# A decoder layer with 32 experts: the first expert's rows get a routing product of their own, and the last tile's bias sum becomes one of the planned tasks

## The chip, the cores and the metric

The kernel runs on 1 core of one Trainium2 chip. The metric is the device time of one execution in microseconds (us); lower is better. Three runs of the kernel before took 1487.82 to 1492.46 us, median 1490.6.

## What is computed

One layer of a decoder on 512 tokens of width 1024, all in float32. First a mixer (gated DeltaNet heads and sliding-window attention heads side by side) whose output is added to x. Then a mixture of experts: 32 experts, each token goes to its best 4. Cut to what matters here:

```python
h = _rmsnorm(x, norm2_w[l]) * (1.0 + scale2) + shift2
logits = xf @ w_router + b_router
top_val, top_idx = lax.top_k(logits, TOP_K)          # 4 of 32 experts per token
gates = jax.nn.softmax(top_val, axis=-1)
hu = xb @ w_up[e] + b_up[e]                          # xb: the rows of expert e
act = x_glu * sigmoid(SWIGLU_ALPHA * x_glu) * (x_lin + 1.0)
ys = act @ w_down[e] + b_down[e]
out = jax.ops.segment_sum(ys * row_gate[:, None], row_tok, num_segments=T)
x = x + gate2 * out
```

## The kernel before, in words

**Two phases.** The first phase computes the mixer and the routing, the second the experts. Between them the engines' orders are joined: what the first phase leaves on an engine's queue stands ahead of the second phase there.

**The first phase is planned.** Every piece of work is a generator that yields tuples of an engine ("P" TensorE, "V" VectorE, "S" ScalarE, "G" GpSimd, "D" a load on SyncE), an assumed cost in us, and buffer tags. `Flow.run` (L154) always picks the step that could start first by these costs, within a slack of 0.1 us the one with the lowest priority number, and emits its instructions. The order on each engine is the order of emission; the instructions then wait for their data with semaphores. A yielded list of keys waits until other tasks have marked them. After each step the next one of the same task becomes ready the engine's assumed latency later (0.12 for TensorE, 0.2 for the others).

**Routing.** The 512 tokens are four tiles of 128 rows. For tile i, `route(i)` (L1258) normalizes the rows, computes the logits, takes the top four (L1311 to L1316, the one-hot sum `ohs`), computes each row's position within its expert with products of TensorE (`pos`, L1320 to L1322), then on VectorE the softmax and the slot numbers (L1325 to L1331), and in `table` (L1179; L1183 to L1192 on VectorE, L1196 on TensorE) a table from slot and expert to token and gate, which is added up over the tiles in `ten` (L1342). `ranks` (L1497) counts the rows of each expert and sorts the experts by count (L1504 to L1517, `perm`); `eri` (L1524) is the list of experts in that order. Expert 0 is always first. `places` (L1529) needs `ten` of all tiles and `perm`: it writes `gi` (L1537), the token numbers of each expert's slots, and the rows and gates of the outputs (L1544 to L1550).

**Bias sums.** `finish(i)` (L1350) multiplies a tile's gates with the experts' down-biases (a transpose L1363, two products L1370, VectorE's product L1373), adds them to the residual rows (L1377, for the last tile on VectorE, else on GpSimd) and stores them to the output (L1381, for the last tile on ScalarE's queue, else on GpSimd's). For tiles 0 to 2 it is a planned task; for the last tile it is run behind the planned phase (L1666).

**The second phase.** Experts go in a fixed order of slots; for each, GpSimd clears a buffer and gathers the rows with an indirect DMA (`gather`, L1685), TensorE transposes them (L1706; VectorE copies the first half, ScalarE the second, L1707), multiplies by the up weights in eight steps (L1755), VectorE and ScalarE compute the activation (L1764 to L1770), TensorE transposes it (L1778), and the down product follows (L1792). TensorE's order is: up of expert q, with the activations of q-1 transposed before its fourth step and the rows of q+1 before its sixth, then down of q-1. Where an expert has few rows, its second unit of 64 rows is skipped in most steps.

**The weights** (1 MB chunks, 8 for up and 4 for down) come through SyncE's queue into a ring of 16 slots. The 12 chunks of the first expert are loaded during the first phase. The second expert's number is copied by GpSimd from `eri` into `second` (L1899), by an order edge behind the first gather, and SyncE reads it (L1877) before it issues that expert's chunks; behind six of them it issues the biases of the first two experts (L1635). For later chunks it waits until TensorE has released a slot.

**Another order edge** (L1903, `behind`) holds the last tile's two stores behind ScalarE's half of the first copy.

Of the kernel before, what the change touches and what calls it, by code (L numbers as in the profile page):

```python
# [12 lines left out]
I32 = mybir.dt.int32  # L13
# [170 lines left out]
def layer_kernel(ctx: ExitStack, tc: tile.TileContext, A, out, probe=None):  # L184
# [111 lines left out]
    def behind(late, early):  # L296

        tc.add_manual_dep(late.ins, early.ins.name,
                          mybir.DependencyInfo(mybir.DependencyClass.NoSync, mybir.DependencyReason.DATA), reason="order")
# [958 lines left out]
    def route(i):  # L1258
# [3 lines left out]
        rt = wk("cv", "rt", 4)  # L1262
        pay, t3, lTs = rt[:, 0:256], rt[:, 0:P].rearrange("p (k e) -> p k e", e=NE), rt[:, P:2 * P]
        cuts = {"at": 256}
        for n, w in (("lo", NE), ("v8", 8), ("g4", 8), ("ss", 4), ("i4", 4)):
            a = cuts["at"]
            cuts[n], cuts["at"] = rt[:, a:a + w], a + w
        lo, v8, g4, ssb, i4 = (cuts[n] for n in ("lo", "v8", "g4", "ss", "i4"))
        oh = oha[:, i]
        yield "N", 0.0, "x"  # L1270
        h2 = wk("x", "h2", 4, D)
# [49 lines left out]
            TE.matmul(pos, lhsT=bc(one, [P, P]), rhs=ohs[:, q], start=(q == 0), stop=False)  # L1321
        TE.matmul(pos, lhsT=C("LT"), rhs=ohs[:, i], start=(i == 0), stop=True)  # L1322
        S.activation(g4[:, 0:4], v8[:, 0:4], AF.Exp, bias=g4[:, 4:5], accum_out=g4[:, 5:6])
        yield "V", 1.0
        V.reciprocal(g4[:, 5:6], g4[:, 5:6])  # L1325
        V.tensor_scalar(slots[:, i, 1], g4[:, 0:4], g4[:, 5:6], None, op0=OP.mult)
# [162 lines left out]
    cnti = const.tile([NE, NE], I32, name="cnti")  # L1489
    ngr = (32 * NBMAX + P - 1) // P  # L1490
    gi = const.tile([P, ngr, NE], I32, name="gi")
    pieces = ((64, NBMAX // 2), (32, (NBMAX + 1) // 2))
    si = {w: const.tile([P, n, NE], I32, name=f"si{w}") for w, n in pieces}
    sg = {w: const.tile([P, n, NE], F32, name=f"sg{w}") for w, n in pieces}
# [65 lines left out]
    with tc.manual_schedule(engines={nc.vector.engine, nc.scalar.engine, nc.tensor.engine, nc.gpsimd.engine, nc.sync.engine}):  # L1560
        columns(rows2, 32, 51)
        for i in range(NT):
            (V.tensor_copy if i % 2 else S.copy)(swt[i // 2][:, i % 2, 0:512], tq[i])
        for i in range(2):
            (V.tensor_copy if i % 2 else S.copy)(swt[i][:, :, 512:768], tkv[i].rearrange("p (i n) -> p i n", n=256))

        def chain(*tasks):
            for t in tasks:
                yield from t

        def swa():
            flow.add(PR["swa"], swa_norms())
            for i in range(NT):
                flow.add(PR["swa"], swa_heads(i))
                for kv in range(2):
                    flow.add(PR["swa"], swa_weights(i, kv))
                    flow.add(PR["swa"] - 1, swa_values(i, kv))
            yield [("norms",)]

        order = [(n, p, c0 + 256 * p) for p in range(2) for n, c0 in (("k", 512), ("q", 0), ("v", 1024))]  # L1580
        flow.add(1, gates())
        wins[512, 0] = wins[512, 1] = w0s
        for hf in range(2):
            flow.mark("win", 512, hf)
        flow.taken.update({"x": 2, "r": 1})
        flow.free["V"] = 1.9
        flow.add(0, chain(*(win(c0) for c0 in [c for _, _, c in order][1:] + [1536, 1536 + 256])))
        flow.add(PR["conv"], chain(*(conv(p, n, c0, PR["cend"]) for n, p, c0 in order)))
        for p in range(2):
            for f in (lengths, decay, turned, inverse, levels):  # L1590
                flow.add(PR["in"] + (f is levels), f(p))
        flow.add(PR["swa"], swa())
        flow.add(1, late_loads())
        flow.add(PR["late"], chain(*(late(r) for r in range(2, 6))))
        flow.add(PR["z"], chain(*(gate(p, PR["z"]) for p in range(2))))
        flow.add(PR["load"], loads())
        flow.add(PR["rec"], recur())
        for i in range(NT):
            flow.add(PR["yS"], out_swa(i))
            flow.add(PR["yT"], out_delta(i))  # L1600
            flow.add(PR["rt"] - 0.2 * i, route(i))
            if i < NT - 1:
                flow.add(PR["fin"], finish(i))
        flow.add(PR["rt"], router_bias())
        flow.add(PR["rt"] - 0.1, ranks())
        flow.add(0, places())
        flow.run()
# [55 lines left out]
    ahead = (load_up(ahead[0]), load_down(ahead[1]))  # L1663

    see("oT", state["oT"].rearrange("p h t -> p (h t)"))
    for _ in finish(NT - 1):  # L1666
        pass
    mix.close()


# [14 lines left out]
    def gather(n, gidx):  # L1685
        xs = []
        for g in range((n + 3) // 4):
            rows_ = 32 * min(4, n - 4 * g)
            xg = moe.tile([P, D], F32, name="xg", bufs=3)
            xs.append((xg, rows_))  # L1690

            G.memset(xg[:rows_], 0.0)  # L1692
            state["gather"] = G.indirect_dma_start(  # L1693
                out=xg[:rows_], out_offset=None, in_=h2d, in_offset=bass.IndirectOffsetOnAxis(ap=gidx(g)[:rows_], axis=0),
                bounds_check=T - 1, oob_is_err=False)
        return xs
# [193 lines left out]

    def rows_of(q):
        r = ORDER[q]
        return gather(NB[r], lambda g: gi[:, g, r:r + 1])

    overflow = overflow_list()
    with tc.manual_schedule(engines={nc.sync.engine, nc.tensor.engine, nc.vector.engine, nc.scalar.engine}):
# [3 lines left out]
        ups = {0: ahead[0], 1: fetch_up(1)}  # L1900
        xs[1] = rows_of(1)
        xT = {0: turn(xs.pop(0))}
        for d in stores[-2:]:  # L1903
            behind(d, state["turned", 1])
        bbs = {0: spread_bias(NB[ORDER[0]], bias[0])}
        acts, pend, last = {}, [], {}
        for q in range(NE + 1):
# [88 lines left out]
```

## Time and profile before

| | |
|---|---|
| median of 3 runs | 1490.6 us (1487.82 to 1492.46) |
| the profiled execution | 1486.96 us, its span 1485.2 us |
| TensorE busy in the span | 1379.4 us (93%) |
| VectorE, ScalarE, GpSimd busy | 563.7, 237.7, 261.1 us |
| moved by DMA | 476.16 MB, 321 GB/s on average |
| mean granted TensorE clock | 0.977 |

The profile's engines are PE (TensorE products), PEld (its weight loads), DVE (VectorE), ACT (ScalarE), POOL (GpSimd) and SP (SyncE, which only issues DMAs here; "SPq" is its queue). Times are in us from the span's start. A row of the timeline gives the start, the duration, engine, line, operation, the tile written and the tiles read, the shape, the count of merged instructions, and in brackets how long the engine had been idle before and what ended that.

### The profile page before, as it was taken

Reading aid. Unit: us, or ns where it says so; the run is one execution under the profiler, and the core shown is the slowest. Engines: PE = TensorE matmul, PEld = TensorE weight load, DVE = VectorE, ACT = ScalarE, POOL = GpSimd, SP = SyncE. Lnnn points to the kernel's source line nnn. Section 1 sums busy time; section 2 is a strip of 40 time slices with the busy share of each in tenths; the row PEclk is TensorE's granted clock in tenths of the full one; section 3 lists DMA queues with packets and bytes.
Section 4 is the critical chain, followed back from the end, with each engine's and each line's share of the span. In section 5 each row is a group of like instructions: output and inputs, shape, how many; then the busy total and the mean of one; then the engine's idle time right before and its main releaser. Section 6 shows DMA issues by size and latency. Waiting matters only on the chain. (4 is left out here: it accounts for less than half of the span.)

```text
span 1485.2 us, 22293 instructions
## 1 busy us (share of the span) xinstructions
PE 1379.4 (93%) x8586; PEld 599.5 (40%) x8586; DVE 563.7 (38%) x1247; ACT 237.7 (16%) x542; POOL 261.1 (18%) x216
## 2 busy tenths in 40 slices
PE   4999999999878999879999999999999999999974
PEld 3766656754443333222233333333333333343311
DVE  7965577566753312212231232222331323232310
ACT  4353354431111000000000000000000000010000
POOL 2213143102331111100011101102010102211010
PEclk9999999999969999999999999999999999999986
DMA  9656210266447999999999999999999999999995
GB/s 304 208 199 213 102 44 15 64 214 269 142 174 287 389 401 404 397 401 415 411 411 400 385 423 402 385 407 397 400 368 364 387 350 405 390 417 415 414 415 236
DMA packets 104980, 476.16 MB, mean 321 GB/s; under 512 B 13992, under 2 KB 39556, under 8 KB 55714
## 3 DMA queue, kind: packets, MB, share of 16 engines
q1 hardware_dynamic: 91842, 453.16, 77.0%
q0 software_dynamic: 11952, 18.75, 5.4%
q10 hardware_dynamic: 1072, 2.70, 0.5%
q8 instruction: 75, 1.23, 0.3%
q14 instruction: 39, 0.32, 0.1%
HBM read 464.14 MB, written 17.22 MB: 324 GB/s over the span
## 5 line engine op out<-in xcount | busy, mean ns | idle before, releaser
L1755 PE MATMUL ps_up<-we,xTe 128*64 128x512 f32 (+1 forms) x3040 | 621.0, 605 | 22.7 <-DMA we<-in_w_up_dram 19.7
L1755 PEld LDWEIGHTS ps_up<-we,xTe 128*64 128x64 f32 (+1 forms) x3040 | 188.0, 132 | 395.5 <-issue 332.7
L1792 PE MATMUL ps_dn<-we,aT 128*64 128x512 f32 (+1 forms) x1848 | 316.9, 535 | 24.5 <-DMA we<-in_w_down_dram 13.9
L1792 PEld LDWEIGHTS ps_dn<-we,aT 128*64 128x64 f32 (+1 forms) x1848 | 103.4, 130 | 239.4 <-issue 185.3
L1800 POOL DMA_INDIRECT out_dram<-yv,si x52 | 81.7, 1571 | 655.0 <-DVE yv L1799 472.9
L1707 DVE COPY xTe<-ps_xTe 128x256 f32<-128x256 f32 (+3 forms) x35 | 17.5, 500 | 309.3 <-PE ps_xTe L1706 309.3
L1780 ACT COPY aT<-ps_aT 128x512 f32<-128x512 f32 (+1 forms) x52 | 26.0, 529 | 517.7 <-PE ps_aT L1778 514.2
L1764 DVE TENSOR_TENSOR hu<-ps_up,bb 128x512 f32<-128x512 f32 (+1 forms) x52 | 32.1, 617 | 200.0 <-PE ps_up L1755 200.0
L1799 DVE SCALAR_TENSOR_TENSOR yv<-ps_dn,sg,g2p 128x512 f32<-128x512 f32 x38 | 28.5, 751 | 193.9 <-PE ps_dn L1792 193.0
L1766 ACT ACTIVATE hu<-hu 128x512 f32<-128x512 f32 (+1 forms) x52 | 29.8, 573 | 271.3 <-DVE hu L1765 271.3
L1692 POOL MEMSET xg<- 64x1024 f32 (+3 forms) x35 | 37.1, 1080 | 188.9 <-PE ps_xTe L1706 188.6
L317 PE MATMUL ps_ch<-hhi,wih 128*128 128x512 f32 x128 | 58.3, 455 | 0.0
L317 PE MATMUL ps_ch<-hl,wih 128*128 128x512 f32 x128 | 50.6, 396 | 0.0
L317 PE MATMUL ps_ch<-hhi,wl 128*128 128x512 f32 x128 | 50.3, 393 | 0.0
L1715 DVE STREAM_SHUFFLE bb<-bias 128x1024 f32<-128x1024 f32 (+1 forms) x44 | 48.6, 1132 | 0.1
L1707 ACT COPY xTe<-ps_xTe 128x256 f32<-128x256 f32 (+3 forms) x35 | 15.2, 433 | 165.2 <-PE ps_xTe L1706 165.2
L1693 POOL DMA_INDIRECT xg<-h2d,gi x35 | 35.8, 1022 | 16.1 <-POOL xg L1692 8.3
L1706 PEld LDWEIGHTS ps_xTe<-cst,xg 64*128 64x128 f32 (+3 forms) x280 | 24.1, 142 | 32.6 <-issue 23.1
L1778 PEld LDWEIGHTS ps_aT<-cst,act 128*128 128x128 f32 x180 | 24.3, 208 | 29.3 <-issue 25.6
L1706 PE MATMUL ps_xTe<-cst,xg 64*128 64x64 f32 (+3 forms) x280 | 30.2, 250 | 5.4 <-DMA xg<-h2d,gi 2.5
L1142 PE MATMUL ps_y<-wos,oS 128*128 128x512 f32 x64 | 33.4, 613 | 0.0
L1778 PE MATMUL ps_aT<-cst,act 128*128 128x128 f32 x180 | 31.2, 304 | 2.3 <-DVE act L1770 1.9
(392 smaller groups left out, 1378.6 us busy)
## 6 DMA issues: line engine op xcount, KB each, us to landing
we<-in_w_up_dram SPq DMA_DIRECT2D x256, 1024.0 KB
we<-in_w_down_dram SPq DMA_DIRECT2D x128, 1024.0 KB
wa<-in_w_ada_dram SPq DMA_DIRECT2D x16, 512.0 KB
wi<-in_w_in_dram SPq DMA_DIRECT2D x8, 1024.0 KB
wl<-in_w_ada_dram SPq DMA_DIRECT2D x12, 512.0 KB
oS<-in_w_ada_dram SPq DMA_DIRECT2D x10, 512.0 KB
LL<-in_w_ada_dram SPq DMA_DIRECT2D x10, 512.0 KB
wt<-in_w_in_dram SPq DMA_DIRECT2D x4, 776.0 KB
```

What stands on the lines that cost most here:

```text
L317: TE.matmul(acc, lhsT=w[a], rhs=x_[b], start=start and q == 0, stop=stop and q == 2)
L1142: TE.matmul(a, lhsT=oS[:, j, P * i:P * i + P], rhs=wo[j][:, 512 * hf:512 * hf + 512], start=(j == 0), stop=(j == 3))
L1692: G.memset(xg[:rows_], 0.0)
L1693: state["gather"] = G.indirect_dma_start(out=xg[:rows_], out_offset=None, in_=h2d, in_offset=bass.IndirectOffsetOnAxis(ap=gidx(g)[:rows_], ...
L1706: TE.transpose(pt[:, k, :rows_], xg[:rows_, 512 * hf + P * k:512 * hf + P * k + P], ident[:rows_, :rows_])
L1707: state["turned", hf] = (S.copy if hf else V.tensor_copy)(xt_[:, 4 * hf:4 * hf + 4, :rows_], pt[:, :, :rows_])
L1715: V.stream_shuffle(bbs[w].rearrange("p h n -> p (h n)"), b[w], [0] * 32)
L1755: TE.matmul(t[w * j:w * j + w], lhsT=lhsT, rhs=rhs, start=(k == 0), stop=(k == KT - 1))
L1764: V.tensor_tensor(g, pg, bbs[w][:, 0], op=OP.add)
L1778: TE.transpose(pt[:, P * a:P * a + P], lv[:, a // 2, a % 2], ident)
L1792: TE.matmul(py[u][w * j:w * j + w, 0:m], lhsT=aT[u][:, kt % nf, w * (kt // nf):w * (kt // nf) + w], rhs=wd[kt][:, m * j:m * j + m], start= ...
L1800: G.indirect_dma_start(out=outv[u[1]], out_offset=bass.IndirectOffsetOnAxis(ap=sidx, axis=0), in_=yv, in_offset=None, compute_op=OP.add, b ...
```

## The change

In `route(i)`, right behind the positions, three VectorE operations take the position of expert 0 (a copy), the token number less that position, and a 128x128 selection matrix: a row has a one at its position if its token chose expert 0. One TensorE product of that matrix with the column gives for each slot the token that belongs there; VectorE adds it over the tiles in `at0`, and the last tile's sum goes, with the slot's own number added, into `gi0`. The first gather reads `gi0` instead of `gi`. `finish` of the last tile becomes a planned task as those of the other tiles, and the order edge that held its stores behind ScalarE's copy is taken out.

```diff
-        for n, w in (("lo", NE), ("v8", 8), ("g4", 8), ("ss", 4), ("i4", 4)):
+        for n, w in (("lo", NE), ("v8", 8), ("g4", 8), ("ss", 4), ("i4", 4), ("k0", 2)):
...
         TE.matmul(pos, lhsT=C("LT"), rhs=ohs[:, i], start=(i == 0), stop=True)
         S.activation(g4[:, 0:4], v8[:, 0:4], AF.Exp, bias=g4[:, 4:5], accum_out=g4[:, 5:6])
+
+        yield "V", 0.4
+        V.tensor_copy(k0[:, 0:1], pos[:, 0:1])
+        V.tensor_scalar(k0[:, 1:2], pos[:, 0:1], -1.0, C("TOKT", i, i + 1), op0=OP.mult, op1=OP.add)
+        sel0 = lTs
+        V.tensor_scalar(sel0, C("IOTA", 0, P), k0[:, 0:1], ohs[:, i, 0:1], op0=OP.is_equal, op1=OP.mult)
+        yield "P", 0.15
+        at = pr[:, 2 * NE + P:2 * NE + P + 1]
+        TE.matmul(at, lhsT=sel0, rhs=k0[:, 1:2], start=True, stop=True)
+        yield "V", 0.1
+        if i == NT - 1:
+            V.scalar_tensor_tensor(gi0, at, C("ROWT"), at0, op0=OP.add, op1=OP.add)
+        elif i:
+            V.tensor_tensor(at0, at, at0, op=OP.add)
+        else:
+            V.tensor_copy(at0, at)
...
+    gi0 = const.tile([P, 1], I32, name="gi0")
+    at0 = ce.tile([P, 1], F32, name="at0")
...
-            if i < NT - 1:
-                flow.add(PR["fin"], finish(i))
+            flow.add(PR["fin"], finish(i))
...
-    for _ in finish(NT - 1):
-        pass
...
-        return gather(NB[r], lambda g: gi[:, g, r:r + 1])
+        return gather(NB[r], lambda g: gi[:, g, r:r + 1] if q else gi0)
...
-        for d in stores[-2:]:
-            behind(d, state["turned", 1])
```

## Rows read from the trace of the kernel before

**Rows 1.** Stages: length, PE, PEld, DVE, ACT, POOL busy, clock, DMA share, GB/s

```profile
700.00:1000.00 300.00, 295.80 (x1646) 101.84 (x1644) 77.77 (x149) 20.46 (x40) 41.27 (x33) 1.00 1.02 404
...
464.30:467.60 3.30, 3.30 (x9) 1.01 (x10) 0.56 (x1) 0.58 (x1) 0.00 (x0) 0.50 0.86 356
...
475.50:481.40 5.90, 5.59 (x26) 1.70 (x22) 2.85 (x6) 0.63 (x1) 0.00 (x0) 1.00 0.00 0
```

**Rows 2.** Timeline of SyncE's queue: start, duration over all issues of the row

```profile
429.50 12.13 SPq L1649 DMA_DIRECT2D we<-in_w_up_dram  x6
...
458.16 27.67 SPq L1649 DMA_DIRECT2D we<-in_w_up_dram  x6
```

**Rows 3.** Waits of SyncE's queue from 340 to 480: total, times, longest

```profile
SPq L1877 <- POOL second L1899: 25.7, 1, 25.7
```

**Rows 4.** Timeline of GpSimd where the second phase begins

```profile
418.20 1.85 POOL L1692 MEMSET xg<- 128x1024 f32 x2
427.16 1.10 POOL L1693 DMA_INDIRECT xg<-h2d,gi  x1 [7.12 <-issue]
428.26 0.18 POOL L1899 COPY second<-eri 1x1 int32<-1x1 int32 x1
```

**Rows 5.** Timeline of all engines, routing of the last tile

```profile
418.15 0.63 PE L1322 MATMUL ps_rt<-sums,cse 128*128 128x32 f32 x2 [0.52 <-DVE rt L1317]
...
418.81 1.26 DVE L1326 TENSOR_SCALAR slots<-rt 128x4 f32<-128x4 f32 x1
...
421.37 0.28 DVE L1183 TENSOR_TENSOR rt<-kS,slots 128x128 f32<-128x128 f32 x1
...
423.31 0.51 DVE L1517 TENSOR_SCALAR ex<-cst,ec,cse 128x32 f32<-128x32 f32 x2
...
424.44 0.42 DVE L1342 TENSOR_TENSOR ten<-ten,ps_rt 128x256 f32<-128x256 f32 x1 [0.34 <-PE ps_rt L1196]
...
424.79 0.17 ACT L1524 CAST eri<-ps_er 32x32 int32<-32x32 f32 x1 [6.20 <-PE ps_er L1522]
...
426.01 0.28 DVE L1537 TENSOR_SCALAR gi<-ps_gi,cse 128x64 int32<-128x64 f32 x1 [0.82 <-PE ps_gi L1535]
```

**Rows 6.** The same timeline, last bias sum and first rows

```profile
428.56 1.22 PE L1370 MATMUL ps_bd<-bdh,fin 96*128 96x512 f32 x2 [0.35 <-ACT fin L1365]
...
430.60 1.28 DVE L1377 TENSOR_TENSOR y<-y,bt 128x512 f32<-128x512 f32 x2
...
432.26 1.97 PE L1706 MATMUL ps_xTe<-cst,xg 128*128 128x128 f32 x8 [2.48 <-DMA xg<-h2d,gi]
433.42 0.69 DVE L1707 COPY xTe<-ps_xTe 128x512 f32<-128x512 f32 x1 [1.54 <-PE ps_xTe L1706]
```

**Rows 7.** The same timeline, routing of tile 2 and an output product

```profile
399.12 0.15 DVE L1325 RECIPROCAL rt<-rt 128x1 f32<-128x1 f32 x1
...
400.49 0.23 DVE L1331 TENSOR_SCALAR slots<-si,cse 128x4 f32<-128x4 int32 x1
...
402.42 1.35 DVE L1183 TENSOR_TENSOR rt<-kS,slots 128x128 f32<-128x128 f32 x1
...
404.30 1.50 PE L1196 MATMUL ps_rt<-room,rt 128*64 128x256 f32 x8 [1.95 <-DVE room L1192]
...
407.60 1.13 PE L1161 MATMUL ps_y<-wod,oT 128*128 128x512 f32 x2
```

**Rows 8.** The same timeline, from the first expert to the second

```profile
453.99 0.01 DVE L1715 LOAD_MASK_SELECT bb<-bias  x1 [19.89 <-DMA bias<-in_b_up_dram]
...
455.53 0.68 DVE L1764 TENSOR_TENSOR hu<-ps_up,bb 128x512 f32<-128x512 f32 x1
...
455.67 5.37 PE L1755 MATMUL ps_up<-we,xTe 128*64 128x512 f32 x24 [1.04 <-DVE xTe L1707]
...
463.64 0.77 PE L1778 MATMUL ps_aT<-cst,act 128*128 128x128 f32 x4 [1.92 <-DVE act L1770]
...
464.33 5.28 PE L1755 MATMUL ps_up<-we,xTe 128*64 128x512 f32 x16
```

More of the change, by code (lines that the diff above doesn't have):

```diff
@@ L1264, in route @@
         cuts = {"at": 256}
-        for n, w in (("lo", NE), ("v8", 8), ("g4", 8), ("ss", 4), ("i4", 4)):
+        for n, w in (("lo", NE), ("v8", 8), ("g4", 8), ("ss", 4), ("i4", 4), ("k0", 2)):
             a = cuts["at"]
             cuts[n], cuts["at"] = rt[:, a:a + w], a + w
-        lo, v8, g4, ssb, i4 = (cuts[n] for n in ("lo", "v8", "g4", "ss", "i4"))
+        lo, v8, g4, ssb, i4, k0 = (cuts[n] for n in ("lo", "v8", "g4", "ss", "i4", "k0"))
         oh = oha[:, i]
```

## The prediction

> **What bounds the kernel now.** I read the table of stages first. From 700 to 1000 us the DMA engines are busy all the time at 404 GB/s: the experts' weights stream, and the end is set by that stream [rows 1]. So a few microseconds can be won only where the stream stands still. It does so from 475.5 to 481.4 us, with 0 GB/s [rows 1], and SyncE's own list says why: of the third expert's eight chunks the last six, from 458.16 on, are spread over 27.67 us [rows 2], because the ring is full and every further chunk waits until TensorE has used up an older one. TensorE's path through the first two experts thus sets the moment from which the stream runs without a break, and **a shift of TensorE at 475 to 485 us is a shift of the end**, one for one. The DMA idles also before 429.5, where SyncE waits 25.7 us for the one number `second` [rows 2, 3], but what that gap costs is only what TensorE later waits for.
>
> Next I followed that path backwards in the timeline. The second expert's products begin at 455.67 after 1.04 us of idling for a VectorE copy (the first expert's end at 454.63); VectorE itself had stood 19.89 us until the first expert's bias landed at 453.99, and started its activations at 455.53 [rows 8]. The second transpose of activations waits 1.92 us for them, until 463.64, and the 16 products behind it take 5.28 us where 24 took 5.37 before [rows 8]: the clock was granted at 0.50, the lower level, from 464.3 to 467.6 [rows 1]. The bias, in turn, is queued on SyncE behind six weight chunks that all wait for `second`, and the first chunk goes out 1.06 us after GpSimd's copy of it ends [rows 2, 4]. GpSimd makes that copy behind the gather of the first rows, at 427.16, which waits for the last tile's table [rows 4, 6]. So the gather's place holds up two things: the rows themselves (TensorE gets them at 432.26 [rows 6]) and the weights and bias.
>
> **The change, part by part.**
>
> The added work for a tile is four VectorE operations and one product. A one-column operation took 0.15 [rows 7], the 128x128 selection lies between that and 0.28 (the 128x128 product of L1183 [rows 5]); together about 0.7 us of VectorE a tile. Tiles 0 and 1 are far from the end and I cost them at nothing: their cover is VectorE's idle time while TensorE does output products, and if it is gone they cost 1.4. Tile 2 has no cover: its table's product (L1196) already kept TensorE 1.95 us waiting for VectorE [rows 7], and the last tile's output products stand behind it. So **+0.7** (bounds 0 and 2.1, plus waits for TensorE, see the rivals).
>
> In the last tile the selection meets a stall that is there already: L1326 took 1.26 us instead of some 0.2 and ended at 420.07, just as GpSimd's two memsets (418.20 for 1.85) ended [rows 4, 5]. The selection stalls in its place, to 420.1, and lasts until 420.3. The product then takes what the position product took, 0.63 [rows 5], and the sum into `gi0` 0.15: ready at 421.1. In that gap VectorE can do the ranks' first three operations, and I expect the ranks' second block (to 423.82 now, 1.0 us) to follow at once, since it becomes ready before the route's next step. Then come L1325 to L1331, 1.6 us as in tile 2 (399.12 to 400.72 [rows 7]), and the table starts at 421.1 + 1.0 + 1.6 = 423.7 instead of 421.37 [rows 5]: **+2.3** for the table, and so for the places of all other experts.
>
> The gather of the first expert comes forward. Now it leaves 0.87 after its index (427.16 [rows 4], where L1537 ends at 426.29 [rows 5]), and with `gi0` at 421.1 + 0.7 it leaves at 422.7 and lands by about 428. GpSimd is free of it 1.1 later, at 423.8. `second` needs the ranks: done at 422.1 instead of 423.82 and no longer behind the table's product, so `eri` stands at about 423.5 (424.96 now [rows 5]). The copy of `second` at 423.8 lets SyncE issue at 425.0 instead of 429.50: **4.5 us earlier** (1.6 if the table keeps its place ahead of the ranks). Of SyncE's queue the fourth chunk still waits for the last reader of the early constants; the second expert needs it only in its fourth step, so that is hidden. The other experts' gathers wait for the table, 3.0 later than now; the first five steps of the first expert cover them, and without that cover they would cost up to 3.0.
>
> The last bias sum moves ahead. Its instructions are the same; before, some of them filled gaps already. From the table's sum (424.86) to the last bias product's end (429.78) TensorE needs 4.92 us [rows 5, 6]. Now all of it precedes the first expert's transposes by order, and they no longer wait for rows: TensorE is free at 424.86 + 2.3 + 0.7 + 4.92 = 432.8 instead of 432.26. VectorE has one more product and one more sum behind that, half of 1.28 each [rows 6], before its copy: 434.1 instead of 433.42. **TensorE starts the first expert about 0.8 late** (bounds: 1.9 early, if the tail packs so that only the rows' landing counts; 2.9 late). The order that held the two stores behind ScalarE's half of the copy is gone: they go out ahead of it, but that half is needed only at the fifth of eight steps, so they cost nothing; without that slack they would cost the wait for VectorE's last y sum, some 1 us.
>
> A memset of GpSimd for the third gather may fall on the y sums of VectorE. The nearest row is L1183 of tile 2, 1.35 instead of 0.28 while GpSimd added [rows 7]; what is left of a memset there would be 0.6 at most. I take 0, since the memset's place isn't fixed, and keep 0.6 for the range. The Trainium skill (SBUF — State Buffer, section "SBUF: two separate sides") says that the port pair of VectorE and GpSimd is an exclusive lock, and that an operation with two SBUF inputs is locked out only by a GpSimd operation that reads SBUF; a memset would then not hold the y sums at all, and the term would be 0.
>
> What comes of it. The bias follows the weights in one queue; 4.5 us earlier it lands near 449.5, and the copy is done before the first expert's products end (454.63 + 0.8 = 455.4). The 1.04 us gap closes. The first unit's result is ready eight products before that end (8 of 24 in 5.37 is 1.8 [rows 8]): 452.8 + 0.8 = 453.6, and VectorE's activations start there instead of at 455.53: 1.9 earlier. The second transpose then comes at 461.7 and no longer leaves TensorE idle but for a moment: the next 16 products start **1.9 us earlier**. If TensorE's gaps at 454.6 and 461 close, the clock need not fall, and 16 products take 16/24 of 5.37 = 3.6 instead of 5.28: **1.7 us** (bounds 0 and 1.7; I take all, as in the row the fall comes right behind these gaps).
>
> Sum: -1.9 - 1.7 = -3.6. Against the profiled execution (1486.96, 3.6 below the median 1490.6) that is 1483.4; against the median, which is what runs will be compared with, **1487.0**.
>
> **The rivals.**
>
> No change: the planner keeps the ranks behind the table, SyncE gains only 1.6, the bias lands at 452.3, its spread and the copy end at 454, and the clock falls all the same. Then 455.53 - 454.0 = 1.5 is left at most, and nothing if the tail is 2.9 late, its bound; the middle, -0.8, gives 1489.8. For it: the clock fell after pauses of this size; against it: the ranks' block is ready first.
>
> Faster: the tail packs, TensorE starts at the rows' landing, 1.9 early, and the activations start 1.9 + 0.8 earlier than in my sum: -3.6 - 2.7 = -6.3, 1484.3. For it: most of the last sum's steps fit into TensorE's and VectorE's waits for ScalarE. Against it: VectorE has more to do in that stretch.
>
> Slower: the sum into `at0` makes VectorE wait for TensorE. Its product stands in TensorE's order behind output products, a pair of which takes 1.13 [rows 7], and behind the waiting sum stand the normalization and output sums of the next tile. In tiles 0 to 2, with up to two pairs ahead and 0.7 of work each, that is 3 x 3.0 = 9 us on the last tile. The gain of the bias and the clock is then outrun: 8.3 beyond my 0.7, less 3.6: +4.7, 1495.3. It decides once the last tile is more than 4.3 later than now. For it: the added wait is real, in every tile; against it: each wait can be filled with work of another task, as the order is planned with it.
>
> **How the numbers follow.** 0.3% is 4.5 us, about what a measurement of this kernel can tell from no change. Chances: my forecast 0.46, no change 0.17, faster rival 0.27, slower rival 0.10. Faster by over 0.3% takes the faster rival and a part of the forecast's spread: 0.33. Slower by over 0.3% is most of the slower rival: 0.08. Within: 0.59. The range reaches below the faster rival by tile 2's 0.7 (bound 0) and by some 1.5 for the spread of the runs (1487.82 to 1492.46), to 1482, and on the other side half-way into the slower one, 1493.
>
> **What would show it.** Right: the first gather near 422 on GpSimd, SyncE's first chunk near 425, the bias landed before 452, no idling before the second expert's products, no stretch at 0.50 near 464, and TensorE's first expert still starting near 435. The last would be wrong if it starts before 432.5 or after 437; the whole is wrong if the last tile's position product (now at 418.15 [rows 5]) comes over 3 us later, or if the standstill before 481 only gets longer by what TensorE gains.

## The result, and the profile after

The changed kernel takes 1507.85 us (median of 4 runs, 1502.06 to 1512.27) beside 1489.21 for the kernel before on the same chip (1486.93 to 1492.46): ratio **1.0109**, 95% interval 1.0086 to 1.0131. I had forecast 1487.0 within 1482 to 1493; it is slower, by 16 us after the ratio and 19 after the medians. The profiled execution took 1507.3 us (span 1505.5), 20.3 more than that of before.

I cut both profiled spans at three instructions that both kernels have: the last transpose of the recurrence's output (L1475 before, L1491 after), the last tile's position product (L1322), and the third expert's first products, where the stream runs again. Each number is a start or a difference of two starts, of the second of the position product's two products (418.38 and 429.22) and of the first of the third expert's; the rows of the last two cuts of after are below.

```
                                       before    after    difference
last recurrence transpose starts at     344.2    346.1     +1.9
to the last tile's position product      74.2     83.1     +8.9
to the third expert's first products     66.9     66.9      0.0
to the end of the span                  999.9   1009.5     +9.6
```

The first difference is of no meaning (another run of the kernel with before's order had 348.0 there). So there are two losses of nine microseconds each, one ahead of all that I had summed and one behind it, and the stretch where I expected a gain of 3.6 stayed as long as it was.

The stages of after (length, busy time of PE, PEld, DVE, ACT, POOL, the granted clock, DMA share, GB/s):

```profile
380.00:393.50 13.50, 9.02 (x65) 5.03 (x65) 11.50 (x36) 3.58 (x11) 2.74 (x3) 1.00 0.31 119
393.50:403.80 10.30, 8.35 (x52) 6.58 (x53) 7.20 (x36) 0.39 (x2) 1.25 (x1) 0.50 0.00 0
...
475.50:478.90 3.40, 3.40 (x10) 0.98 (x8) 0.12 (x1) 0.32 (x1) 0.00 (x0) 0.50 0.95 381
...
700.00:1000.00 300.00, 294.22 (x1662) 100.75 (x1658) 77.71 (x150) 21.57 (x42) 41.77 (x34) 1.00 1.02 400
```

The same two stages of the kernel before, which its rows ahead of the prediction don't show:

```profile
380.00:393.50 13.50, 12.38 (x63) 5.89 (x61) 12.50 (x40) 2.92 (x9) 2.21 (x3) 1.00 0.50 161
393.50:403.80 10.30, 8.38 (x48) 4.59 (x46) 9.08 (x27) 1.86 (x8) 4.99 (x4) 1.00 0.48 181
```

TensorE does 9.02 us of work instead of 12.38 before 393.5, and then works at the lower clock for 10 us, where before it had the full one. In the middle of the stream the DMA engines are as busy as in [rows 1] but move 400 GB/s instead of 404. The fall of the clock of [rows 1] and [rows 8] is still there, at 475.5.

GpSimd's timeline of after, over the stretch of [rows 4]:

```profile
429.59 1.92 POOL L1708 MEMSET xg<- 128x1024 f32 x2 [7.30 <-DMA h2d<-h]
432.39 1.10 POOL L1709 DMA_INDIRECT xg<-h2d,gi  x1 [0.89 <-POOL xg L1708]
437.15 2.78 POOL L1698 MEMSET bias<- 128x512 f32 x4 [3.66 <-PE ps_rt L1196]
439.87 0.18 POOL L1915 COPY second<-eri 1x1 int32<-1x1 int32 x1
```

The first gather leaves 3.4 us behind the start of the position product (428.99), sooner than the 4.5 I had (9.0 in [rows 4, 5]). But `second`, which I put right behind it, stands behind four clearings of the bias buffers, and these wait 3.66 us for TensorE's table product. In the kernel before they came last:

```profile
435.51 0.95 POOL L1693 DMA_INDIRECT xg<-h2d,gi  x1 [0.27 <-POOL xg L1692]
436.47 2.79 POOL L1682 MEMSET bias<- 128x512 f32 x4
```

So SyncE's first chunk, of [rows 2], goes out at 441.11, 12.1 us behind that start, where it was 11.4. VectorE and TensorE of after, the rows that answer to [rows 5, 6, 8]:

```profile
428.99 0.64 PE L1322 MATMUL ps_rt<-sums,cse 128*128 128x32 f32 x2
...
430.67 0.59 PE L1332 MATMUL ps_rt<-rt 128*128 128x1 f32 x2 [0.41 <-DVE ec L1528]
...
443.81 1.50 PE L1722 MATMUL ps_xTe<-cst,xg 128*128 128x128 f32 x8
...
496.08 1.49 PE L1771 MATMUL ps_up<-we,xTe 128*64 128x512 f32 x6
```

```profile
429.86 0.76 DVE L1329 TENSOR_SCALAR rt<-cst,rt,sums 128x128 f32<-128x128 f32 x1
...
431.30 0.22 DVE L1335 SCALAR_TENSOR_TENSOR gi<-ps_rt,cse,at 128x1 int32<-128x1 f32 x1 [0.44 <-PE ps_rt L1332]
...
433.98 0.29 DVE L1183 TENSOR_TENSOR rt<-kS,slots 128x128 f32<-128x128 f32 x1
...
437.40 2.58 DVE L1374 CAST fin<-sums 128x64 fp32r<-128x64 f32 x1
```

The last tile's own steps come about as summed: the index is written 2.3 us behind that start, the table begins 5.0 behind it (3.2 in [rows 5], so +1.8 for the +2.3 I gave). New is the cast of the last bias sum: 2.58 us instead of 0.19, for as long as the clearings run on GpSimd.

### The profile page after: what moved, and what is told of

The parts are those of the page before. It is cut to its first block, busy times and chain, and to the rows that moved or that the text cites. A ratio compares the mean times of both kernels' runs of the same rounds, so it can differ in the third digit from the quotient of the medians.

```text
span 1505.5 us, 22323 instructions
## 1 busy us (share of the span) xinstructions
PE 1388.8 (92%) x8594; PEld 601.5 (40%) x8594; DVE 567.7 (38%) x1263; ACT 237.9 (16%) x542; POOL 260.6 (17%) x216
## 3 DMA queue, kind: packets, MB, share of 16 engines
q1 hardware_dynamic: 91842, 453.16, 76.6%
## 5 line engine op out<-in xcount | busy, mean ns | idle before, releaser
L317 PEld LDWEIGHTS ps_ch<-hhi,wih 128*128 128x128 f32 x128 | 24.2, 189 | 23.1 <-issue 18.0
```

Source lines behind the costliest of these rows:

```text
L317: TE.matmul(acc, lhsT=w[a], rhs=x_[b], start=start and q == 0, stop=stop and q == 2)
```

## The experiments

Theories for the tile phase: **P**, the three steps that the change gives the planner make it order tiles 0 to 2 differently, TensorE idles and its clock falls; **W** (my slower rival), the instructions themselves and VectorE's wait for the product. For the stream: **A**, the new tile of 32 bytes shifts the addresses of the weight slots behind it; 13 of the 16 stood at multiples of 256 bytes, the last three at 224 beyond one (the addresses are those of the built programs), and in the profile of before, going by the order of the packets, these three held most of the 313 ns packets. Rivals stand with each run. Ratios are to the kernel before on the same chip; I give 1% as 14.9 us.

**An unused tile in the kernel before.**

```diff
     gi = const.tile([P, ngr, NE], I32, name="gi")
+    pad = const.tile([P, 1], I32, name="pad")
```

> The kernel before with an unused 32-byte tile at the place where the change puts the first expert's rows; nothing else differs, and the order of work is the same. It moves 13 of the 16 weight slots by 32 bytes, from multiples of 64 to 32 beyond one. Theory A (the address of a slot sets what its packets cost; in the profile of before only the three slots at 32 beyond a multiple of 64 show packets of 313 ns beside 309): ratio 1.005 to 1.007, +8 to +10 us; mean 8192-byte packet 322 to 323 ns instead of 319.6. Rival (the slower stream of the changed kernel comes from its later start or from the chip of the day): ratio within 0.999 to 1.001, mean packet 319.6 ns.

Measured: 1500.07 us, ratio 1.0064 (1.0039 to 1.0088), mean packet 322.7 ns. Theory A holds: no instruction differs, and 9.5 us are lost. Its stage shows the changed kernel's 400 GB/s:

```profile
700.00:1000.00 300.00, 294.14 (x1644) 101.20 (x1638) 78.10 (x151) 21.00 (x41) 40.72 (x33) 1.00 1.02 400
```

**The changed kernel with 64 bytes.**

```diff
-    gi0 = const.tile([P, 1], I32, name="gi0")
+    gi0 = const.tile([P, 16], I32, name="gi0")[:, 0:1]
```

> The changed kernel with that one tile widened from 32 to 64 bytes a partition, so that the 13 slots are at multiples of 64 again; no instruction differs. Theory A (addresses): 8 to 10 us less than the changed kernel, ratio to the kernel before 1.004 to 1.006 (1495 to 1498 us), mean packet near 319.6 ns; the standstill of the stream still ends near 496 us. Rival (not the addresses): the ratio stays near 1.011.

Measured: 1504.23 us, ratio 1.0085 (1.0065 to 1.0105), mean packet 323.1 ns. The theory as I put it, with 64 bytes, fell: a multiple of 64 is no better than 32 beyond one.

**The instructions in the old order.** In tiles 0 to 2 the added work has no steps of its own; `gi0` has 64 bytes.

```diff
-        yield "V", 0.4
+        yield "V", 0.4 if i == NT - 1 else 1.0
...
-        yield "P", 0.15
-        TE.matmul(at, lhsT=sel0, rhs=k0[:, 1:2], start=True, stop=True)
...
         pay, sum_ = table(i, 0, pay, [lambda: room[0], lambda: room[1]])
+        if i < NT - 1:
+            TE.matmul(at, lhsT=sel0, rhs=k0[:, 1:2], start=True, stop=True)
         sum_(pte)
```

> The changed kernel with the 64-byte tile, and in tiles 0 to 2 the added instructions put inside steps that are there already (VectorE's part into the step behind the position product, the product and the sum into the table's and its sum's steps), so that the planner orders all tiles as in the kernel before; the instructions and the last tile are as changed. Theory P (the planner's new order of tiles 0 to 2 and the clock that falls with it made the last tile late): the last tile's position product comes at 418 to 420.5 us instead of 429.0, no fall of the clock at 393, and the time is 9 to 13 us below that of the changed kernel with the 64-byte tile, 1482 to 1489 us. Theory W, my slower rival (the instructions themselves, with VectorE waiting for the product): the position product stays above 425 us and the time above 1494.

Measured: 1499.71 us, ratio 1.0059 (1.0039 to 1.0079), 4.5 below the run before; no fall of the clock before 418. The position product's row:

```profile
419.98 0.64 PE L1322 MATMUL ps_rt<-sums,cse 128*128 128x32 f32 x2 [1.09 <-DVE rt L1317]
```

In the profile it comes 7.8 us earlier than with 64 bytes and the new order, as theory P has it; the time, still with slots off their places, fell by less than the 9 to 13 that I had named.

**The new order without the instructions.**

```diff
+        yield "V", 0.4
+        yield "P", 0.15
+        yield "V", 0.1
         yield "V", 1.0
```

> The kernel before with three empty steps in each tile's routing, of the planned costs that the change gives its own (0.4 on VectorE, 0.15 on TensorE, 0.1 on VectorE), and no instruction added; so the order of tiles 0 to 2 is that of the changed kernel, with none of its work, and the first gather, its index and the last bias sum are as before. Theory P (order and clock): the last tile's position product comes at 424 to 429 us, a fall of the clock between 385 and 412 as in the changed kernel, and the time is 5 to 12 us above before. Theory W (the instructions and VectorE's waits): the position product stays at 417 to 420 us and the time within 2 us of before.

Measured: 1497.26 us, ratio 1.0041 (1.0027 to 1.0055). The position product and the stage:

```profile
424.76 0.64 PE L1322 MATMUL ps_rt<-sums,cse 128*128 128x32 f32 x2
```

```profile
380.00:393.00 13.00, 8.76 (x75) 5.14 (x73) 11.35 (x34) 2.98 (x10) 2.47 (x3) 1.00 0.28 105
393.00:399.70 6.70, 6.14 (x34) 4.31 (x35) 6.35 (x26) 0.00 (x0) 0.91 (x1) 0.50 0.00 0
```

Three empty steps, and TensorE idles and falls to the lower clock as in the changed kernel: 80.5 us from the recurrence to the position product instead of 74.2. In the traces TensorE's and VectorE's instructions up to that product come in the changed kernel's order here, the added ones aside, and in before's order in the folded runs. Theory P carries 6.3 of the 8.9 us; the other 2.6 go with the added instructions in that order, by one profile of this run, while before's own order gave 74.2 to 77.0 (last table). What the lower clock has of the 6.3 and what the idling was not tried.

**Which multiple.** The kernel before with a tile of 128 bytes, and with the last three slots brought to multiples of 256 too:

```diff
+    pad = const.tile([P, 32], I32, name="pad")
```

> The kernel before with an unused tile of 128 bytes at the place of the change's own, so that 13 of the 16 weight slots, which stood at multiples of 256, stand 128 beyond one (four small tiles of a loop that runs no pass share one tile, to make room). With 32 bytes the ratio was 1.0064, and a tile of 64 bytes did not mend the changed kernel. Theory A128 (a slot must start at a multiple of 128): ratio 0.999 to 1.001, mean 8192-byte packet 319.6 to 320.0 ns. Theory A256 (it must be 256): 1.005 to 1.007 and 322.4 to 323.1 ns. Rival (any shift of these tiles costs, whatever the address): also 1.005 to 1.007, and then the kernel with all slots at multiples of 256 gains nothing.

```diff
+    gap = room_for("gap").tile([P, 56], F32, name="gap")
     ringo, hup, actp, moe, aTp, ringy, moel, misc = (room_for(n) for n in ("ringo", "hu", "act", "moe", "aT", "ringy", "moel", "misc"))
...
-        ts = misc.tile([P, 1], F32, name="ts", bufs=1)
+        few = gap[:, 0:8]
+        ts = few[:, 0:1]
```

> The kernel before with its last three weight slots moved down by 224 bytes, so that all 16 stand at multiples of 256 (a tile of that size goes ahead of them and takes up the small tiles of the loop that runs no pass). Theory A (the address sets the packets' cost): packets of 313 ns all but go, mean 319.6 less some 0.6 ns, and the time 1.5 to 2.5 us below before (3 of 13 of the 9 us), ratio 0.998 to 0.999. Rival (any shift costs): 1.000 to 1.002.

Measured: 1498.0 us, 1.0045 (1.0029 to 1.0061), for the first; 1488.79 us, **0.9979** (0.9967 to 0.9992), for the second. Theory A256 holds: 128 is not enough (though time and packets lie a little under what I had named for it), and the last three slots, moved to a multiple, gain. The weight packets of 8192 bytes (the last 49152 of the execution; mean over 560 to 1400 us), from the DMA records:

```
kernel               13 slots  3 slots   packets of   mean
                     (bytes beyond       309 ns       ns
                     a multiple of 256)
before                   0       224       39841      319.6
after                   32       224       20198      322.7
before, 32 bytes        32       224       19953      322.7
after, 64 bytes         64       224       21589      323.1
before, 128 bytes      128       224       26459      322.2
before, all at 256       0         0       41626      319.4
```

3.1 of 319.6 ns is 1.0%, and 1.0% of the 1000 us behind the standstill is the 9.6 us of the first table. At 64 and 128 bytes the two agree less well: 1.1 and 0.8% by the packets, 7.5 and 7.6 us in that stretch.

What the last three slots gain the mean hardly shows: I had named some 0.6 ns less, it is 0.2, and the changed kernel with before's addresses (next run) has 319.4 as well. Two other counts do. Packets of 312 to 314 or 319 to 321 ns fall from 3.8% to 0.8% (the changed kernel has 39.5%), and the stretch behind the third expert's start took 997.6 to 998.2 us in the three profiles with all slots at multiples, 998.4 to 1001.9 in the nine with before's addresses (last table). Ten times the slow packets for five times the slots off their places: whether that comes of the offset or of the number of such slots was not tried.

**The changed kernel, addresses mended.** Two one-number tiles share one, which makes room for `gi0`.

```diff
-    ntot = const.tile([1, 1], I32, name="ntot")
+    ones2 = const.tile([1, 8], I32, name="ones2")
+    ntot, second = ones2[:, 0:1], ones2[:, 1:2]
...
-    second = const.tile([1, 1], I32, name="second")
```

> The changed kernel with the 32 bytes of its new tile won back by letting two one-number tiles share one, so that all weight slots keep the addresses of before; no instruction differs. Theory A: mean packet 319.6 to 320.0 ns, ratio 1.0035 to 1.0055, about 9 us less than the changed kernel; the stream's standstill still ends near 496 us, 10.8 later than before, and nearly all that is left of the loss is that. Rival (the slower packets come from something else in the change): the ratio stays near 1.011 and the packets near 322.7 ns.

Measured: 1496.66 us, ratio 1.0036 (1.0023 to 1.005), mean packet 319.4 ns. Theory A holds. Of the 10.9 us between 1.0109 and 1.0036 the profiles put 10.0 behind the third expert's start (495.15), the addresses; the stretch before that is 2.0 shorter too, since there the clock did not fall as it had at 475.5 (16 products take 3.65 us instead of 5.35).

**Clearings behind the second gather**, with the instructions folded and the addresses mended:

```diff
-    for b in bias:
-        for t in b.values():
-            G.memset(t, 0.0)
...
+        xs[1] = rows_of(1)
+        for b in bias:
+            for t in b.values():
+                behind(G.memset(t, 0.0), state["gather"])
         ups = {0: ahead[0], 1: fetch_up(1)}
-        xs[1] = rows_of(1)
```

> The run with the instructions folded into steps of the old order, with all weight slots at the addresses of before, and with GpSimd's four clearings of the bias buffers put behind the second gather instead of ahead of the copy of second. Theory M (the clearings, queued ahead of that copy and falling on a VectorE cast, are what took the local gain away): the copy ends near 425 us and SyncE's first chunk goes out near 426.3 instead of 432.4; the cast takes 0.2 us; the first expert's products start near 435.5 instead of 438.1, the stream's standstill ends at 484 to 486 us instead of 487.5, and the time is within 3 us of before, ratio 0.998 to 1.001. Rival (rows and the last bias sum hold the first expert anyway): the standstill ends at 487 us or later as before, ratio 1.001 to 1.002 even with the addresses mended.

Measured: 1488.42 us, ratio **0.9978** (0.9964 to 0.9992). This profile's position product came late (425.9, a fall of the clock at 410.6 among the reasons), so the instants that I had named are all some 5 us later, and the distances count: `second` 4.6 us behind it instead of 9.9, the standstill's end 62.4 instead of 66.9. (As an instant that end, 488.3, lay where the rival had it, at 487 or later; in the second profile of this kernel, further down, it lay at 483.7.) GpSimd and VectorE:

```profile
429.41 1.10 POOL L1711 DMA_INDIRECT xg<-h2d,gi  x1 [1.85 <-issue]
430.51 0.18 POOL L1917 COPY ones<-eri 1x1 int32<-1x1 int32 x1
```

```profile
434.43 0.19 DVE L1379 CAST fin<-sums 128x64 fp32r<-128x64 f32 x1
```

(The tile that the copy now shares stands as `ones`, its number left out.) TensorE goes from the first expert into the second without a pause, and the clock stays up, as the prediction had it; these answer to [rows 8] and to the stage of 464.3 in [rows 1]:

```profile
457.95 9.64 PE L1773 MATMUL ps_up<-we,xTe 128*64 128x512 f32 x44
467.52 1.51 PE L1796 MATMUL ps_aT<-cst,act 128*128 128x128 f32 x8
```

```profile
464.30:467.60 3.30, 3.30 (x17) 1.12 (x13) 3.20 (x7) 0.63 (x1) 0.00 (x0) 1.00 1.02 429
```

The clock needed less than that, though. In the kernel before with 32 bytes TensorE idled 0.20 us for the copy and still 1.91 for the activations, and the 16 products behind ran at the full clock:

```profile
457.16 5.37 PE L1756 MATMUL ps_up<-we,xTe 128*64 128x512 f32 x24 [0.20 <-DVE xTe L1708]
...
465.12 0.75 PE L1779 MATMUL ps_aT<-cst,act 128*128 128x128 f32 x4 [1.91 <-DVE act L1771]
465.80 3.65 PE L1756 MATMUL ps_up<-we,xTe 128*64 128x512 f32 x16
```

So it was with the empty steps and with the addresses mended (0 and 0.28 us for the copy, 1.92 for the activations). In the five profiles with 0.55 to 1.04 us for the copy and the same 1.92, before and the change among them, these products took 5.25 to 5.35 us, with 0.50 granted for 3.4 of it.

The same with the clearings where the change puts them, and the changed kernel's own order with the clearings moved:

> The run with the added instructions folded into steps of the old order and the weight slots at the addresses of before, with GpSimd's clearings of the bias buffers left where the change put them (ahead of the copy of second). Against the run with the clearings behind the second gather it tells what they cost. Theory M: ratio 0.9995 to 1.001, some 3 us above that run's 0.9978; from the last tile's position product to the end of the stream's standstill 66 to 67.5 us, where that run took 62.4; the cast of the last bias sum takes over 2 us. Rival (the clearings cost nothing, the rest is the spread of runs): ratio 0.997 to 0.999, and the stretch 62 to 64 us.

> The changed kernel in its own order of tiles, with the weight slots at the addresses of before and GpSimd's clearings behind the second gather. Theory: addresses and clearings mended, what is left is the planner's order of tiles 0 to 2 (last tile 7 to 11 us late) less the local gain of 3 to 4: ratio 1.000 to 1.002, 3 us or more below the run with the addresses alone (1.0036), and 3 to 6 above the folded run (0.9978). Rival (the order of tiles costs nothing by itself): within 0.001 of the folded run.

Measured: 1493.82 us, 1.0018 (1.0002 to 1.0035), and 1494.1 us, 1.0025 (1.0012 to 1.0037). In the first the cast takes 2.58 us again, 65.9 us lie between position product and third expert, and theory M holds, the time a little above its range and the stretch 0.1 short of it. In the second the stretch is 62.3 us, so the clearings give there what they gave in the folded run; the time is only 1.6 us below 1.0036, where I had named 3 or more, and 7.0 above 0.9978. By ratios the clearings cost 6.0 us in the folded pair (3.6 against that run's repetition, further down) and 1.6 in the other, whose intervals overlap; by profiles 3.5 and 2.6. Their size is known no better than that.

```profile
431.81 2.58 DVE L1379 CAST fin<-sums 128x64 fp32r<-128x64 f32 x1
```

**The two halves alone.** The last bias sum in the list and no product; and the folded run with the last bias sum left behind the phase:

```diff
-            if i < NT - 1:
-                flow.add(PR["fin"], finish(i))
+            flow.add(PR["fin"], finish(i))
```

> The kernel before with the other part of the change alone: the last tile's bias sum joins the list of tasks and its two stores are no longer held back; no product of its own for the first rows, slots at the addresses of before. My sum: some steps of that sum fill waits already and the rows of the first gather still come last, so within 1.5 us of before, ratio 0.999 to 1.001. Rival 1 (it is what moves GpSimd's clearings ahead of the copy of second): that copy 2 us or more later against the last tile's position product than the 9.9 us of before, ratio 1.001 to 1.003. Rival 2 (it is the part that gains): below 0.998.

> The folded run with clearings behind the second gather, less one half of the change: the last tile's bias sum stays behind the phase, with the two stores held back as before. It tells which half brings the local gain. Theory S (the gain is the earlier gather, copy of second and chunks, which the product alone brings): 62 to 64 us from the last tile's position product to the end of the standstill, ratio 0.9975 to 0.9995. Rival (the last bias sum must go ahead of the first expert for it): 65 us or more, ratio 1.000 or more.

Measured: 1493.74 us, 1.0017 (1.0004 to 1.0029), for the first: Rival 1. This half alone moves the clearings ahead of the copy, which comes 12.6 us behind the position product (the cast of the bias sum takes 0.19 us here, so the 68.4 us of the stretch, 66.9 before, owe nothing to it):

```profile
431.73 1.10 POOL L1690 DMA_INDIRECT xg<-h2d,gi  x1 [7.12 <-PE ps_sl L1544]
432.82 2.80 POOL L1679 MEMSET bias<- 128x512 f32 x4
435.54 0.68 POOL L1896 COPY second<-eri 1x1 int32<-1x1 int32 x1
```

For the second, 1490.19 us, 1.0002 (0.9989 to 1.0015), and 64.0 us: the stretch speaks for theory S, with 2.9 of the 4.5 us from the product alone. The time is just above the range I gave it, where the rival had it; its tile phase took 79.9 us.

**All together.** First with the gap of the run above, which moves the tile of the first gather by 224 bytes too; then with the gap at the far end from the first tile on, so that nothing moves against anything else; and the folded run again beside it:

> All that helped together: instructions folded into the old order, clearings behind the second gather, and all 16 weight slots at multiples of 256. If the two gains add (0.9978 and 0.9979 each by itself): ratio 0.9950 to 0.9965, near 1485 us. If they do not add: 0.997 to 0.999.

Measured: 1491.78 us, 1.0005 (0.999 to 1.0019). The gains do not add there. The first gather's tile lay now on 224 bytes of the last tile's routing table, and its clearing waited for that:

```profile
433.73 1.88 POOL L1711 MEMSET xg<- 128x1024 f32 x2 [7.69 <-PE ps_rt L1196]
435.78 1.10 POOL L1712 DMA_INDIRECT xg<-h2d,gi  x1 [0.17 <-POOL xg L1711]
```

```diff
+    gap = ctx.enter_context(tc.tile_pool(name="gap", bufs=1, side="right")).tile([P, 56], F32, name="gap")
     mo = mix.enter_context(tc.tile_pool(name="mo", reuse_waits="tile", bufs=2, side="right"))
```

> All that helped, once more, without what spoiled it last time: the 224 bytes that bring all 16 weight slots to multiples of 256 now lie at the far end of the right side from the first tile on, so that the tile of the first gather lies on the same earlier tiles as before (last time it also lay on the last tile's routing table, and its clearing waited for that until 433.7 us). Theory: standstill's end 62 to 63 us behind the last tile's position product, the rest of the time behind it 997.5 to 998.5 us instead of 1001, ratio 0.9950 to 0.9970. If the parts still do not add: 0.998 or more.

> The folded run with clearings behind the second gather and the addresses of before, unchanged, beside the two others on their chip: 62 to 63 us from the position product to the end of the standstill, 1000.5 to 1002 behind it, ratio 0.996 to 0.9995 as the first time (0.9978).

Measured: 1485.97 us, **0.9972** (0.9958 to 0.9987), and 1488.49 us, 0.9994 (0.9979 to 1.0008). The first is the fastest of all, 4.2 us below the kernel before, and just beyond the range I named; 61.6 us to the third expert and 998.1 behind it. So the moved tile was the cause. (For room, two small tiles of the routing lie in its working tile in that run.) Its interval overlaps with those of the folded run, the second of which gave less than the first (0.9978), so that the two gains add is seen in the profile and not proved by the times.

```profile
421.48 1.86 POOL L1710 MEMSET xg<- 128x1024 f32 x2
425.20 1.10 POOL L1711 DMA_INDIRECT xg<-h2d,gi  x1 [1.85 <-issue]
426.30 0.18 POOL L1917 COPY ones<-eri 1x1 int32<-1x1 int32 x1
```

All profiled executions, cut as in the first table (us):

```
                               tile phase   to the third   behind it   ratio
                                            expert
before                            74.2         66.9          999.9
the change                        83.1         66.9         1009.5     1.0109
 64 bytes                         83.6         67.1         1007.4     1.0085
 addresses mended                 83.4         64.9          999.5     1.0036
 and clearings late               83.5         62.3         1001.9     1.0025
empty steps alone                 80.5         67.2         1000.5     1.0041
folded, 64 bytes                  76.0         67.3         1008.1     1.0059
folded, addresses                 77.7         65.9         1001.1     1.0018
 and clearings late               79.9, 77.7   62.4, 61.9   1001.2, 998.4  0.9978, 0.9994
 and all slots at 256             77.7         61.6          998.1     0.9972
  first gather's tile moved        79.9         67.2          997.6     1.0005
 product alone                    79.9         64.0          999.2     1.0002
last bias sum alone               77.0         68.4         1001.0     1.0017
before, 32 bytes                  74.2         66.4         1010.9     1.0064
before, 128 bytes                 74.2         66.1         1007.5     1.0045
before, all slots at 256          76.6         66.2          998.2     0.9979
```

## Why the prediction was wrong

**What bounds the kernel** held. The table shows it: what the tile phase or the stretch to the third expert loses or gains is found again in the span, while the stream behind it takes its 998 to 1002 us, or 1007 to 1011 with shifted slots.

**The step that failed first: "Tiles 0 and 1 are far from the end and I cost them at nothing", with +0.7 for tile 2.** I counted instructions and not the steps that carry them. Three new steps in a list that is planned by costs reorder the work of all tiles; that alone cost 6.3 us in the profile and 1.0041 in time. My slower rival had the size right (9 us on the last tile; 8.9 came) by the wrong mechanism: VectorE's waits for the product are not what costs the most, the order is. And what I set against that rival, "the order is planned with it", was the cause. Folded into old steps the added work still cost more than my 0.7: 1.8 us in the one profile without an early fall of the clock, 3.5 in the three where it was granted at 0.50 for 3.4 us from 368 to 370 on, and 5.7 in the three where it fell at 408 to 411 as well. That second fall came in two runs without the instructions too (76.6 and 77.0), the first in none; why the folded work brings it was not tried.

**The step that failed second: "GpSimd is free of it 1.1 later, at 423.8 ... The copy of `second` at 423.8 lets SyncE issue at 425.0".** I went through what GpSimd waits for, not through all that it has queued. The clearings of the bias buffers are unordered work, they stood last before, and moving the last bias sum into the list brought them ahead. They also held the cast. With them moved, `second` comes 4.6 us behind the position product (my 423.8 stood 5.4 behind it).

**What was not in the sum at all** is the stream, 9.5 to 10.9 us. I had read the change's new tile as storage without a price. The Trainium skill (DMA: Bandwidth & Descriptors, section "How a descriptor splits into AXI transactions") says that when a descriptor does not start at a multiple of 256 bytes, its first piece starts at the boundary below, and the bytes fetched in vain take beats of the bus; I had not weighed it. The page tells this of what is fetched, and here the place written to moved. Of the places tried (0, 32, 64 and 128 bytes beyond, and 224 in three slots) only multiples of 256 were free, as a rule of that kind would have it. The size is another: by that page's 32-byte beats a start 32, 64 or 128 bytes beyond would cost, as an estimate from it, 1, 2 or 4 beats in 256, so 0.4, 0.8 or 1.6%, while the mean packets of 322.7, 323.1 and 322.2 ns against 319.6 are 1.0, 1.1 and 0.8%.

**The sum for the stretch from the position product to the third expert was right once nothing stood in its way.** There I had -4.3 (-3.6 less the 0.7 ahead of it); measured -4.5, -5.0 and -4.5 in the three runs that had both halves of the change, the clearings moved and before's addresses. The bias gap closed and the clock stayed up, as said: in the first of them the 16 products behind the second transpose of activations start 2.9 earlier (I had 2.6) and take 1.6 less (I had 1.7). That the clock's term came in full is in part luck: I tied it to both of TensorE's gaps, and it came as well in the three runs above where the second stayed open. One term of it was worse than I had it: SyncE's fourth chunk waits 7.1 us for VectorE's `si`, the last reader of the early constants, which I called hidden; the bias stands behind it in the queue and landed 32.7 us behind the position product instead of 35.6, so 2.9 earlier, where I had 4.5. It was enough. Two slips were small: 434.1 less 433.42 is 0.7 us and not 0.8, and the selection, which I put below 0.28, takes 0.34 where nothing holds it.

```profile
SPq L1895 <- POOL ones L1917: 23.4, 1, 23.4
SPq L1672 <- DVE si L1574: 7.1, 1, 7.1
```

**The memset term.** I looked at the y sums, and the row hit was the cast, with 2.4 us over its 0.19. The Trainium skill (SBUF — State Buffer, section "SBUF: two separate sides") has the pair of ports locked for a VectorE operation in a mode that uses both or with two SBUF inputs; the cast has one SBUF input, and it stood still until the clearings ended. That agrees with the page if the cast runs in such a mode, which no run here shows by itself.

The chance of 0.08 for slower was too small for another reason: the planned order and the layout are two places where any edit can reach all of the kernel, and I gave neither a case.

## What to carry to other kernels

An edit to a planned or listed kernel is first a new order and a new layout: compare the order of instructions on each engine and the addresses of the big buffers before pricing what was added. Small work is best put inside steps that are there, and work that no order binds (here the clearings) has to be given its place, or it moves. Put the buffers of a bandwidth-bound stream at multiples of 256 bytes; here 32 bytes ahead of them cost 0.6%.

## What was unexpected in the hardware

- An 8192-byte packet into SBUF took 309 ns at a multiple of 256 bytes, and with most slots 32 bytes beyond one, some 40% of the packets took 312 to 314 or 319 to 321; 128 bytes beyond a multiple was hardly better (322.2 ns mean) than 32 (322.7).
- A cast of 128x64 on VectorE took 2.58 us instead of 0.19 beside four clearings of 2.78 us on GpSimd, in two kernels; one of 128x128 (the selection, L1329) took 0.76 instead of 0.34 beside another clearing.
- The same order of the same instructions had its tile phase at 74.2 us in three profiles and at 76.6 and 77.0 in two, in which the clock had fallen at 407 to 409 already and not first at 413 to 417. What decides that stays open.
